# Modulation matmuls in a decoder step: column strips taken four at a time

## The chip, the cores and the metric

The kernel runs as one program on one core of a Trainium2 chip. Its time is device microseconds from a timed run; three runs were made of the kernel before. One further execution was profiled, and all rows below come from that one.

## The reference, cut to what matters

A two-layer decoder step runs on 1024 prompt tokens and 8 sample tokens. Layer 0 mixes tokens by retention and by an attention that is restricted to the highest index scores; layer 1 by a gated delta rule. Each layer has an MLP. Each sub-layer's input and output are modulated by vectors that depend on nine conditioning rows (one of the prompt, eight of the samples):

```python
sc = jax.nn.silu(c)
for l in range(DEPTH):                      # DEPTH = 2
    mod = (sc @ p['ada_w'][l] + p['ada_b'][l])[:, None, :]
    sh_m, sc_m, gt_m, sh_f, sc_f, gt_f = jnp.split(mod, 6, axis=-1)
```

`ada_w[l]` is 1024 x 6144 in fp32, so a layer's modulation reads 25.2 MB of weights to make 9 x 6144 numbers. The shift and scale of the first mixer are needed before anything else; the other four of layer 0 by the end of its mixer, and all six of layer 1 by the end of the first MLP.

## The kernel before, in words

Features lie on partitions and tokens on the free axis. Every projection goes through `mm3` (L185), which multiplies exact high and low parts of the weights and of the input: three matrix products for each of 8 (or 4) slices of the contraction, over three blocks of tokens, `BLK` (384, 384 and 264 columns). `_one` makes one block of a tile of 128 output features; `dense` runs over tiles, either block by block (`blk_major`) or tile by tile.

The modulation is made in the background by a generator, `ada` and `_ada` (L313 to L339). A group g of 2048 output columns has 16 half slices of the weights, each of 128 x 1024 (512 KB), loaded by SyncE (L320) into a ring of tiles. The stationary operand is the 32-column tile `scT` of the conditioning rows. So a product with 512 moving columns fills only a strip of 32 columns of the array and 32 partitions of the PSUM bank `ps`; the four strips of a bank are the four 512-column parts of the group. Each `next` on the generator emits one load and the two strips of the load before it. An fp32 strip shows in the trace as two matmul records, so a step is four records. After the last slice the bank is copied (L330), turned (L333) and added to the bias (L339).

Where the steps go is set by the tile-by-tile branch of `dense`:

```python
if b < self.pace:
    next(self.back, None)
```

`pace` is 3 from the even mixer on, so a step follows each block. Three stretches of the kernel run these steps. In the set-up, group 0 of layer 0 runs with nothing else, over a ring of six tiles. In the even mixer's projections (`even_proj`), groups 1 and 2 of layer 0 run between the blocks of the projections AK, AV, two heads of AQ, and the first retention head's RQ, RK, RV and RG, over a ring of two tiles, `N[6]` and `N[12]`; what is left is emitted by `drain` in the middle of `ret_head` (L988). In the first MLP, all three groups of layer 1 run between its blocks, over a ring of three tiles.

The program text is not the order of the queues: a planner in the framework lists the instructions by their place in the text and by when it expects their inputs, and puts each on its engine's queue; each engine then runs its queue in that order and waits where an input is late. SyncE's queue holds the weight loads (L172), the modulation loads, the half swaps of the rotary step (L720, L721) and the spills of the residual (L399).

Other users of the tiles that the change touches: `N[11]` is `on`, which holds the rectified index scores (L844 to L851) and later the outputs of `ret_head`; `N[13]` is `scr` in the sample scores (read by L1280) and `sall`, the retention states, in `ret_head`. Both are ring tiles of the input norm before that. `N[6]` is part of the residual until it is spilled. The search for the highest index scores (`search_init`, L1149 to L1219) runs on VectorE and ScalarE along with the projections, two of its steps emitted after each tile.

Of the kernel before, what the change touches and what calls it, by code (L numbers as in the profile page):

```python
# [44 lines left out]
def _constants():  # L45
    """Tables that follow from the shapes alone."""
# [51 lines left out]
class _Ring:  # L98
    """Tiles handed out in turn."""
# [15 lines left out]
class _Carve:  # L115
    """Small tiles out of one."""
# [15 lines left out]
class _Step:  # L132
    def __init__(self, nc, tc, a, taps=None, stop=None):
        self.nc, self.tc, self.a, self.taps, self.stop = nc, tc, a, taps, stop
        self.ahead, self.pace, self.back, self.under, self.jobs = 1, 1, iter(()), [], []
        self.lanes, self.beat = ([], []), 0
# [5 lines left out]
    # ---------------------------------------------------------------- helpers  # L142
# [5 lines left out]
    def consts(self, i, t):  # L148
        """Load the constants of part i (0 everywhere, 1 even mixer, 2 odd mixer) into tile t."""
        c0, c1 = _CUTS[i], _CUTS[i + 1]  # L150
        self.cst[i] = t[:, :c1 - c0]
        self.nc.gpsimd.dma_start(self.cst[i], self.a['cst'][:, c0:c1])
# [4 lines left out]
    def banks(self, **kw):  # L157
        """Name PSUM banks by role for the code that follows."""
# [19 lines left out]
    def mm3(self, out, w, ms, X, ks, c0, c1, start=True, stop=True):  # L178
        """out[m, c0:c1] of W^T X with W and X as exact high and low parts."""
# [12 lines left out]
    def dense(self, tiles, blk_major, X=None, ks=range(8), after=None):  # L192
        """tiles: (load, m, evac); evac(block, psum). Block by block, after(block) follows each block."""
# [11 lines left out]
        else:  # L205
            self.settle()
            for t in tiles:
                w, off = t[0]()
                for b in range(3):
                    self._one(w, off, t[1], t[2], b, X, ks)  # L210
                    if b < self.pace:
                        next(self.back, None)
                    self.work(1 + b // 2)

    def work(self, n=1 << 30):
        """Emit n steps of the jobs in line."""
# [5 lines left out]
    def tick(self):  # L222
        """Emit a step of one of the two lanes in turn."""
# [6 lines left out]
    def finish(self, g):  # L230
        """Emit all of the lane of g up to its end."""
# [5 lines left out]
    def drain(self):  # L237
        """Emit what is left of the work in the background."""
# [10 lines left out]
    def rsqrt(self, out, x, n, m, scr=None):  # L249
        """out = x ** -0.5 for x [n, m] (a first guess from the bits of x, then Newton's method)."""  # L250
# [10 lines left out]
    # ---------------------------------------------------------------- set-up  # L261
# [17 lines left out]
    def vectors(self):  # L279
        """Per-feature vectors laid on partitions: ada_b (2 x 48), ln_g, ln_b (2 x 2 x 8 each) and others."""  # L280
# [3 lines left out]
        nc.sync.dma_start(ab, a['ada_b'].rearrange("l (j p) -> (l j) p", p=128))  # L284
        nc.sync.dma_start(gn[64:68], a['ret_gn'][0])
        nc.sync.dma_start(gn[68:69], a['odd_gn'])
        nc.sync.dma_start(cw, a['odd_conv'][0].rearrange("w (j p) -> (w j) p", p=128))
        nc.sync.dma_start(gn[0:32], a['ln_g'].rearrange("l s (j p) -> (l s j) p", p=128))
        nc.sync.dma_start(gn[32:64], a['ln_b'].rearrange("l s (j p) -> (l s j) p", p=128))
# [16 lines left out]
    def ada(self, l, gs, ring):  # L306
        """Modulations 2g and 2g+1 of layer l for g in gs, features on partitions, one column per conditioning
        row; a generator, a step to a load."""
# [4 lines left out]
    def _ada(self, l, g, ring):  # L313
        nc = self.nc
        ps = self.side('a')
        raw = {}
        for i in range(17):
            if i < 16:
                raw[i] = ring()
                nc.sync.dma_start(raw[i], self.a['ada_w'][l, 64 * i - i % 2 * 64:64 * i - i % 2 * 64 + 128,  # L320
                                                          2048 * g + i % 2 * 1024:2048 * g + i % 2 * 1024 + 1024])
            if i:
                kt, hf = (i - 1) // 2, (i - 1) % 2
                for c in range(2):
                    j = 2 * hf + c
                    nc.tensor.matmul(ps[32 * j:32 * j + 32, :], self.scT[:, kt, :],  # L326
                                     raw[i - 1][:, 512 * c:512 * c + 512], start=kt == 0, stop=kt == 7)
# [6 lines left out]
        # column block of (quarter q, sub j) is 16 g + 4 q + j  # L334
# [9 lines left out]
    def coefs(self, l_ln, s_ln, l, i):  # L344
        """hf = n * HS + HB with HS = g (1 + scale), HB = b (1 + scale) + shift; resid = n * RA + RB."""
# [18 lines left out]
    # ---------------------------------------------------------------- norm and modulation  # L364
    def weave(self, n):
        """Emit n steps of the norms that are under way."""
# [5 lines left out]
    def settle(self, b=2):  # L372
        """Emit all of the norms up to block b."""
# [3 lines left out]
    def spread(self, b, ns, co, to_dram, ring):  # L377
        """Natural token tiles ns of block b -> resid^T and the split modulated input XH, XL; in steps."""
# [22 lines left out]
    def spread_samples(self, v, co):  # L401
        """v [128, 8, 8], the samples with features on partitions -> resS and the last columns of XH, XL."""
# [14 lines left out]
    def normed(self, b, ring, out, final):  # L417
        """Token tiles of block b of the residual sum, normalised, tokens on partitions; in steps."""
# [44 lines left out]
    def normed_samples(self, ring, then):  # L463
        """The samples' residual sum, normalised, features on partitions; in steps."""
# [42 lines left out]
    def final_samples(self, v):  # L507
        """The samples' normalised rows, scaled, out."""
# [30 lines left out]
    # ---------------------------------------------------------------- residual sum of a projection  # L539
# [22 lines left out]
    def out_proj(self, w, l, after):  # L562
        """resid + (1 + gate) * (X^T w), X the mixer's output."""
# [11 lines left out]
    # ---------------------------------------------------------------- MLP  # L575
# [52 lines left out]
    def arena(self, cp):  # L628
        """The tiles that every phase takes its own from."""
# [8 lines left out]
    def renew(self, x, slots, dt=F32):  # L638
        """Tiles of slots of x anew: what holds float32r parts holds nothing else."""
# [9 lines left out]
    def ev_rings(self):  # L649
        """Tiles of a norm and of the MLP."""  # L650
# [9 lines left out]
    # ---------------------------------------------------------------- whole step  # L660
    def run(self, stop=None):
        nc, tc, a = self.nc, self.tc, self.a
        with tc.tile_pool(name='cp', bufs=1) as self.cp, tc.tile_pool(name='sm', bufs=2) as self.sm, \
# [17 lines left out]
            for _ in range(6):  # L681
                next(self.back)
            self.vectors()
# [3 lines left out]
            for l in range(2):  # L687
# [17 lines left out]
                if l == 0:  # L705
                    self.back = self.ada(1, range(3), _ring(*[t[:, :1024] for t in N[8:10] + [W[9]]]))
# [7 lines left out]
    # ---------------------------------------------------------------- even mixer  # L714
    def rope(self, raw, tabs, half, out, sw=None):
        """out = raw * cos + (halves of raw swapped) * signed sin."""
# [9 lines left out]
    def natural(self, src, out, tag, scale=None, rows=128):  # L726
        """src [rows, >= 1024] (features on partitions) -> out [128, 8, rows] (tokens on partitions)."""
# [14 lines left out]
    def sample_rows(self, src, out, tag, rows=128, scale=None):  # L742
        """The sample columns of src -> out [8, rows]."""
# [22 lines left out]
    def even_proj(self, mis, w, S, SS, aqS, akS, avS, aqD, akD, vD):  # L766
        """Projections, index scores, retention and the search; returns its tiles, the soonest free first."""
# [4 lines left out]
        adw = _ring(N[6], N[12])  # L772
        self.back, self.pace = self.ada(0, (1, 2), adw), 3
# [32 lines left out]
        # indexer queries, keys and weights  # L806
# [28 lines left out]
        # index scores of the prompt rows that have more than 256 keys  # L835
# [19 lines left out]
        # indexer keys out  # L855
# [9 lines left out]
        def aq_tile(h):  # L865
            """A head of queries, turned and sent to DRAM block by block."""
# [44 lines left out]
        # retention  # L911
# [42 lines left out]
    def ret_head(self, h, qT, kT, vT, vn, kn, rg, sall, on):  # L954
        """Retention of the prompt for a head, in steps."""
        nc = self.nc
        vv, kk = [x[:, :NP].rearrange("p (c r) -> p c r", c=8) for x in (vn, kn)]
# [30 lines left out]
        self.drain()  # L988
# [1016 lines left out]
```

## Time and profile before

| what | value |
|---|---|
| three timed runs | 3057.4, 3058.06 and 3073.36 us; median 3058.06 |
| span of the profiled execution | 3055.5 us |
| TensorE busy, share of the span | 2971.4 us, 97% |
| VectorE busy | 1665.6 us, 55% |
| modulation weights read | 96 loads of 512 KB |

The span runs from the first to the last instruction of the profiled execution; the median of the timed runs is 2.6 us above it. Busy time of TensorE is a sum over records whose ends are modelled and which overlap, so 97% busy does not mean that it streams columns 97% of the time.

### The profile page before, as it was taken

The numbers are of one execution on the slowest core, as the hardware profiler recorded it, in microseconds if no ns is written. First come the engines' busy times: TensorE is split into PE (matmuls) and PEld (weight loads), VectorE is DVE, ScalarE is ACT, GpSimd is POOL, SyncE is SP. The second block draws the span as 40 slices with busy tenths as digits, with TensorE's granted clock in tenths as the row PEclk, the third lists the DMA queues.
The fourth block names the chain that finished last, engine by engine and source line by source line (L and its number), as shares of the span: only waits on it lengthen the run. The fifth ranks groups of instructions, "written<-read, shape, count | busy, mean of one in ns | idle before, by whom it ended". The sixth has DMA issues, their size and how long they took to land.

```text
span 3055.5 us, 49859 instructions
## 1 busy us (share of the span) xinstructions
PE 2971.4 (97%) x20052; PEld 2736.0 (90%) x20052; DVE 1665.6 (55%) x4531; ACT 1093.7 (36%) x2240; POOL 188.6 (6%) x248
## 2 busy tenths in 40 slices
PE   8999999999999999999999999999999999999997
PEld 5577997898679999999888999999999999999996
DVE  4678895447223333333677766765575333333337
ACT  4467724425021112222365555552243221112221
POOL 0300003000000000000011111111000000000002
PEclk9999999999999999999999999998999999999998
DMA  8664226102642111111132222233311111111111
GB/s 290 187 184 145 85 78 202 48 28 63 188 156 73 49 49 43 48 49 43 52 91 52 56 54 56 51 115 109 124 56 42 43 48 49 46 45 49 44 40 63
DMA packets 257908, 251.59 MB, mean 82 GB/s; under 512 B 46262, under 2 KB 227291, under 8 KB 257164
## 3 DMA queue, kind: packets, MB, share of 16 engines
q1 hardware_dynamic: 243596, 200.38, 22.2%
q0 software_dynamic: 14080, 48.03, 4.9%
q8 instruction: 157, 2.57, 0.3%
q14 instruction: 75, 0.61, 0.1%
HBM read 207.23 MB, written 37.92 MB: 80 GB/s over the span
## 4 chain that ended last, share of the span: by engine, by line
PE 78%; DVE 11%; ACT 3%; DMA 3%; issue 3%; POOLq 0%; SPq 0%; POOL 0%; DVEq 0%; ACTq 0%
PE bank L185 63%; PE bank L326 3%; DVE wlo L174 1%; DVE W L1471 1%; PE bank L1326 1%; PE bank L1312 1%; PE bank L1839 1%; PE bank L386 1%; ACT whi L173 1%; PE bank L1523 1%; DVE st L437 1%; DMA N<-gcD 1%; DVE N L1530 1%; ACT N L450 1%; PE bank L1633 1%
## 5 line engine op out<-in xcount | busy, mean ns | idle before, releaser
L185 PE MATMUL bank<-XH,whi 128*128 128x384 f32 (+3 forms) x2832 | 942.9, 333 | 5.3 <-ACT whi L173 1.6
L185 PE MATMUL bank<-XL,whi 128*128 128x384 f32 (+3 forms) x2832 | 919.7, 325 | 0.0
L185 PE MATMUL bank<-XH,wlo 128*128 128x384 f32 (+3 forms) x2832 | 919.2, 325 | 0.0
L185 PEld LDWEIGHTS bank<-XH,whi 128*128 128x128 f32 (+2 forms) x2832 | 535.5, 189 | 37.0 <-issue 16.1
L185 PE MATMUL bank<-W,whi 128*128 128x384 f32 (+1 forms) x2304 | 543.0, 322 | 11.6 <-DVE N L593 7.3
L185 PEld LDWEIGHTS bank<-XH,wlo 128*128 128x128 f32 (+2 forms) x2832 | 534.8, 189 | 8.7 <-issue 5.9
L185 PEld LDWEIGHTS bank<-XL,whi 128*128 128x128 f32 (+2 forms) x2832 | 535.9, 189 | 7.2 <-issue 3.9
L550 DVE SCALAR_TENSOR_TENSOR N<-bank,G,N 128x384 f32<-128x384 f32 (+1 forms) x432 | 247.0, 572 | 497.9 <-PE bank L185 497.9
L185 PEld LDWEIGHTS bank<-W,whi 128*128 128x128 f32 x2304 | 394.5, 188 | 40.7 <-DVE N L550 15.7
L173 ACT CAST whi<-raw 128x1024 fp32r<-128x1024 f32 x166 | 172.7, 1040 | 674.4 <-PE bank L185 655.4
L185 PE MATMUL bank<-W,wlo 128*128 128x384 f32 (+1 forms) x1152 | 367.3, 319 | 0.0
L174 DVE TENSOR_TENSOR wlo<-raw,whi 128x1024 fp32r<-128x1024 f32 x166 | 202.7, 1221 | 145.1 <-ACT whi L173 135.8
L593 DVE SCALAR_TENSOR_TENSOR N<-bank,N 128x384 f32<-128x384 f32 (+1 forms) x192 | 98.4, 513 | 295.9 <-ACT N L592 295.7
L592 ACT ACTIVATE N<-bank 128x384 f32<-128x384 f32 (+1 forms) x192 | 87.5, 456 | 368.8 <-PE bank L185 368.8
L185 PEld LDWEIGHTS bank<-W,wlo 128*128 128x128 f32 x1152 | 216.3, 188 | 0.0
L185 PE MATMUL bank<-W,W 128*128 128x384 f32 (+1 forms) x768 | 180.8, 322 | 0.0
L185 PE MATMUL bank<-XH,W 128*128 128x384 f32 (+1 forms) x480 | 155.5, 324 | 1.2 <-DVE N L593 1.2
L185 PE MATMUL bank<-XL,W 128*128 128x384 f32 (+1 forms) x480 | 154.5, 322 | 0.0
L185 PE MATMUL bank<-XH,N 128*128 128x384 f32 (+1 forms) x480 | 154.3, 321 | 0.0
L185 PEld LDWEIGHTS bank<-W,W 128*128 128x128 f32 x768 | 132.4, 188 | 8.6 <-DVE N L550 5.0
L185 PE MATMUL bank<-W,N 128*128 128x384 f32 (+1 forms) x384 | 123.2, 321 | 0.0
L1157 ACT ACTIVATE N<-N,M 128x384 bf16<-128x384 f32 (+3 forms) x128 | 106.2, 830 | 31.1 <-DVE M L1154 27.1
(582 smaller groups left out, 3903.9 us busy)
## 6 DMA issues: line engine op xcount, KB each, us to landing
N<-in_ada_w_dram SPq DMA_DIRECT2D x64, 512.0 KB, 3.8
raw<-in_mlp_up_dram SPq DMA_DIRECT2D x64, 512.0 KB, 4.0
raw<-in_mlp_down_dram SPq DMA_DIRECT2D x64, 512.0 KB, 3.3
W<-in_ada_w_dram SPq DMA_DIRECT2D x32, 512.0 KB, 4.9
raw<-in_odd_w_in_dram SPq DMA_DIRECT2D x32, 512.0 KB, 4.1
raw<-in_even_w_in_dram SPq DMA_DIRECT2D x24, 512.0 KB, 6.3
N<-resD SPq DMA_DIRECT2D x16, 512.0 KB, 4.2
resD<-N SPq DMA_DIRECT2D x4, 1536.0 KB, 7.2
```

The lines of the kernel that those rows point to most:

```text
L173: nc.scalar.copy(hi[:, :k * m], raw[:, :k * m])
L174: nc.vector.tensor_tensor(lo[:, :k * m], raw[:, :k * m], hi[:, :k * m], op=OP.subtract)
L185: self.nc.tensor.matmul(out, ww[:, i, ms], xx[:, c0:c1], start=start and i == 0 and j == 0, stop=stop and i == nk - 1 and j == 2)
L326: nc.tensor.matmul(ps[32 * j:32 * j + 32, :], self.scT[:, kt, :], raw[i - 1][:, 512 * c:512 * c + 512], start=kt == 0, stop=kt == 7)
L386: nc.tensor.transpose(ps[:, 128 * i:128 * i + 128], n[:, 128 * ft:128 * ft + 128], self.ident)
L437: nc.vector.bn_stats(st[:, i, :], zs[i])
L450: nc.scalar.activation(x[:, y], zz[j][i], AF.Identity, scale=rs[:, j:j + 1], bias=nb[:, j:j + 1])
L550: nc.vector.scalar_tensor_tensor(r, ps[:, :w], g[:, dt, 0:1], r, op0=OP.mult, op1=OP.add)
L592: nc.scalar.activation(r, ps[:, :w], AF.Relu)
L593: nc.vector.scalar_tensor_tensor(h, ps[:, :w], 0.0, r, op0=OP.max, op1=OP.mult)
L1157: nc.scalar.activation(ja[:, :n], S[r], AF.Sign, bias=nff[:, r - 2:r - 1], accum_out=cnt[:, r - 2:r - 1])
L1312: nc.tensor.matmul(p[:, :kw], q[:, h], akT[:, k0:k0 + kw], start=True, stop=True)
```

## The change

A step of the generator now takes a whole slice of 128 rows: it emits the four strips of the bank, of two loaded tiles, and the two loads of a later slice. A group has 8 such steps in place of 16. The last strip is emitted first, and the other three are put behind it on the engine's queue. The ring is filled ahead, by half as many slices as it has tiles. `dense` counts slices of contraction and takes a step whenever `every` of them have passed: 8 in the even mixer (a step for each block, as before), 24 in the MLP (a step for each tile of `mlp_up`, and for every two of `mlp_down`). The rings have four tiles in the even mixer (`N[6]`, `N[12]`, `N[11]`, `N[13]`) and four in the MLP. `drain` moves from the middle of `ret_head` to its start. `vectors` becomes a generator whose six small loads are issued by ScalarE, ahead of the first modulation steps, and whose transposes follow after three of them. The rest of the diff removes comments.

```diff
     def dense(self, tiles, blk_major, X=None, ks=range(8), after=None):
...
-                    if b < self.pace:
+                    self.since += len(ks)
+                    if self.since >= self.every:
+                        self.since = 0
                         next(self.back, None)
...
     def vectors(self):
-        nc.sync.dma_start(ab, a['ada_b'].rearrange("l (j p) -> (l j) p", p=128))
...
+        nc.scalar.dma_start(ab, a['ada_b'].rearrange("l (j p) -> (l j) p", p=128))
...
+        yield
         p = self.side()
...
     def _ada(self, l, g, ring):
         nc = self.nc
         ps = self.side('a')
-        raw = {}
-        for i in range(17):
-            if i < 16:
-                raw[i] = ring()
-                nc.sync.dma_start(raw[i], self.a['ada_w'][l, 64 * i - i % 2 * 64:64 * i - i % 2 * 64 + 128,
-                                                          2048 * g + i % 2 * 1024:2048 * g + i % 2 * 1024 + 1024])
-            if i:
-                kt, hf = (i - 1) // 2, (i - 1) % 2
-                for c in range(2):
-                    j = 2 * hf + c
-                    nc.tensor.matmul(ps[32 * j:32 * j + 32, :], self.scT[:, kt, :],
-                                     raw[i - 1][:, 512 * c:512 * c + 512], start=kt == 0, stop=kt == 7)
+        raw = []
+
+        def load(kt):
+            raw.append([ring(), ring()])
+            for hf in range(2):
+                nc.sync.dma_start(raw[kt][hf], self.a['ada_w'][l, 128 * kt:128 * kt + 128,
+                                                               2048 * g + 1024 * hf:2048 * g + 1024 * hf + 1024])
+        n = len(ring.t) // 2
+        for kt in range(n):
+            load(kt)
+        yield
+        for kt in range(8):
+            def strip(j):
+                return nc.tensor.matmul(ps[32 * j:32 * j + 32, :], self.scT[:, kt, :],
+                                        raw[kt][j // 2][:, 512 * (j % 2):512 * (j % 2) + 512], start=kt == 0, stop=kt == 7)
+            with self.tc.issue_after(strip(3).ins):
+                for j in range(3):
+                    strip(j)
+            if kt + n < 8:
+                load(kt + n)
             yield
...
             self.back = self.ada(0, (0,), adw)
-            for _ in range(6):
+            vectors = self.vectors()
+            next(vectors)
+            for _ in range(4):
                 next(self.back)
-            self.vectors()
+            for _ in vectors:
+                pass
             self.drain()
...
                 if l == 0:
-                    self.back = self.ada(1, range(3), _ring(*[t[:, :1024] for t in N[8:10] + [W[9]]]))
+                    self.back, self.every = self.ada(1, range(3), _ring(*[t[:, :1024] for t in N[8:11] + [W[9]]])), 24
...
-        adw = _ring(N[6], N[12])
-        self.back, self.pace = self.ada(0, (1, 2), adw), 3
+        adw = _ring(*[t[:, :1024] for t in (N[6], N[12], N[11], N[13])])
+        self.back = self.ada(0, (1, 2), adw)
...
     def ret_head(self, h, qT, kT, vT, vn, kn, rg, sall, on):
         nc = self.nc
+        self.drain()
...
         nc.gpsimd.dma_start(self.a['ret_prompt'][0, 0, h], sall[:, 7])
-        self.drain()
```

## Rows read from the trace of the kernel before

**Rows 1.** The page, part 1 (busy time) and part 4 (chain that ended last).
```profile
PE 2971.4 (97%) x20052; PEld 2736.0 (90%) x20052; DVE 1665.6 (55%) x4531; ACT 1093.7 (36%) x2240; POOL 188.6 (6%) x248
...
PE 78%; DVE 11%; ACT 3%; DMA 3%; issue 3%; POOLq 0%; SPq 0%; POOL 0%; DVEq 0%; ACTq 0%
```
**Rows 2.** Windows of L326 alone, even mixer and first MLP: window, length, PE busy (records).
```profile
90.00:293.00 203.00, 34.70 (x128) 4.74 (x128) 1.00 0.60 178
755.00:940.00 185.00, 51.54 (x192) 7.04 (x192) 1.00 0.54 168
```
**Rows 3.** Timeline of TensorE round one step in the even mixer: start, length, instruction.
```profile
89.99 0.34 PE L185 MATMUL bank<-XH,wlo 128*128 128x384 f32 x1
90.25 1.05 PE L326 MATMUL bank<-N,scT 128*32 128x512 f32 x4
91.24 0.39 PE L185 MATMUL bank<-XH,whi 128*128 128x264 f32 x1
91.46 0.29 PE L185 MATMUL bank<-XL,whi 128*128 128x264 f32 x1
```
**Rows 4.** Windows of L185 alone: MLP with steps, MLP without: PE (x) PEld (x).
```profile
771.43:930.79 159.36, 119.73 (x685) 107.00 (x684) 1.00 0.55 172
1186.30:1277.80 91.50, 90.99 (x576) 90.67 (x576) 1.00 0.16 47
```
**Rows 5.** The same window of L326 alone.
```profile
771.43:930.79 159.36, 45.24 (x172) 6.19 (x172) 1.00 0.55 172
```
**Rows 6.** Chain in 755 to 945 us, shares by line.
```profile
by line: PE bank L185 74.1%; PE bank L326 25.3%; PE bank L333 0.7%
```
**Rows 7.** Windows: PE, PEld, DVE, ACT, POOL busy (x), clock, DMA share, GB/s.
```profile
90.00:166.00 76.00, 74.14 (x300) 36.86 (x300) 45.43 (x85) 35.85 (x72) 25.91 (x46) 1.00 0.59 184
166.00:292.00 126.00, 125.65 (x740) 98.58 (x738) 105.74 (x299) 91.77 (x198) 4.37 (x9) 1.00 0.60 174
292.00:440.00 148.00, 142.06 (x931) 137.52 (x928) 136.58 (x446) 74.54 (x166) 7.29 (x10) 0.97 0.28 79
440.00:482.00 42.00, 41.65 (x299) 41.27 (x297) 34.29 (x108) 12.56 (x27) 8.50 (x13) 1.00 0.48 141
```
**Rows 8.** Timeline of TensorE where two steps fall together, in the drain.
```profile
269.70 1.07 PE L326 MATMUL bank<-N,scT 128*32 128x512 f32 x8
270.69 0.49 PE L996 MATMUL bank<-W,W 128*128 128x128 f32 x2
```
**Rows 9.** DMA in 166 to 265 us: packets, the hardware queue, then L320's landings.
```profile
DMA packets 10791, 16.91 MB, mean 171 GB/s; under 512 B 792, under 2 KB 7712, under 8 KB 10784
...
q1 hardware_dynamic: 10112, 14.70, 53.0%
...
N<-in_ada_w_dram SPq DMA_DIRECT2D x18, 512.0 KB, 4.3
```
**Rows 10.** DMA in 10 to 40 us (set-up).
```profile
DMA packets 4885, 10.17 MB, mean 339 GB/s; under 512 B 387, under 2 KB 2696, under 8 KB 4884
...
W<-in_ada_w_dram SPq DMA_DIRECT2D x10, 512.0 KB, 6.1
```
**Rows 11.** Last uses of the new ring tiles: VectorE's index-score line, TensorE's L1280.
```profile
L851 DVE SCALAR_TENSOR_TENSOR N<-N,M,N x30: 350/750/753, 105.0 to 142.8; 128x512 f32<-128x512 f32 x18, 128x384 f32<-128x384 f32 x6, 128x128 f32<-128x128 f32 x3, 128x256 f32<-128x256 f32 x3
...
161.53 1.04 PE L1280 MATMUL bank<-N,N 32*32 32x512 f32 x2
```
**Rows 12.** Windows of the set-up, columns as in rows 7.
```profile
10.00:20.00 10.00, 6.47 (x27) 1.12 (x25) 0.97 (x9) 0.00 (x0) 0.00 (x0) 0.87 0.91 291
20.00:30.00 10.00, 9.25 (x34) 1.13 (x28) 0.00 (x0) 0.04 (x1) 0.00 (x0) 0.79 1.02 406
30.00:40.00 10.00, 6.53 (x26) 5.29 (x27) 6.42 (x13) 5.76 (x10) 0.00 (x0) 0.72 0.95 320
```
**Rows 13.** Timeline of TensorE in the set-up.
```profile
18.20 8.01 PE L326 MATMUL bank<-W,scT 128*32 128x512 f32 x24 [2.11 <-DMA W<-in_ada_w_dram]
```
**Rows 14.** SyncE's queue: L320's waits (ns min/median/max), and two issues in order.
```profile
L320 SPq EVENT_SEMAPHORE  x90: 17/17/6437, 11.1 to 926.4; - x90
...
91.35 0.39 SPq L320 DMA_DIRECT2D N<-in_ada_w_dram  x1
...
98.15 0.44 SPq L172 DMA_DIRECT2D raw<-in_even_w_in_dram  x1
```

More of the change, by code (lines that the diff above doesn't have):

```diff
@@ L134, in __init__ @@
         self.nc, self.tc, self.a, self.taps, self.stop = nc, tc, a, taps, stop
-        self.ahead, self.pace, self.back, self.under, self.jobs = 1, 1, iter(()), [], []
+        self.ahead, self.every, self.since, self.back, self.under, self.jobs = 1, 8, 0, iter(()), [], []
         self.lanes, self.beat = ([], []), 0
@@ L283, in vectors @@
         ab, gn, cw = [self.W[9][:n, 128 * i:128 * i + 128] for i, n in enumerate((96, 69, 96))]
-        nc.sync.dma_start(ab, a['ada_b'].rearrange("l (j p) -> (l j) p", p=128))
[L285 to L289, printed above, removed]
+        nc.scalar.dma_start(ab, a['ada_b'].rearrange("l (j p) -> (l j) p", p=128))
+        nc.scalar.dma_start(gn[64:68], a['ret_gn'][0])
+        nc.scalar.dma_start(gn[68:69], a['odd_gn'])
+        nc.scalar.dma_start(cw, a['odd_conv'][0].rearrange("w (j p) -> (w j) p", p=128))
+        nc.scalar.dma_start(gn[0:32], a['ln_g'].rearrange("l s (j p) -> (l s j) p", p=128))
+        nc.scalar.dma_start(gn[32:64], a['ln_b'].rearrange("l s (j p) -> (l s j) p", p=128))
+        yield
         p = self.side()
```

## The prediction
> **What bounds the kernel now.** I read the page first. TensorE is busy 97% of the span and holds 78% of the chain that ended last; VectorE holds 11% [rows 1]. So the question is whether TensorE is the bound in the stretches where the modulation runs, and what it spends there on modulation. L326 outside the set-up is 128 records in 90 to 293 us and 192 in 755 to 940 us [rows 2]; four records are a step, so 32 and 48 steps.
>
> The timeline shows what a step is [rows 3]. The four records are two strips in two passes. They fill 90.25 to 91.24, 0.99 us, in which the dense products stand still. Dense products follow each other every 91.50 / 576 = 0.159 us in a stretch without steps [rows 4]. From the start of the last dense product before the step (89.99) to the second after it (91.46) are 1.47 us, in which two would have needed 0.32: the step costs 1.15 us. A check over a long stretch: 159.36 us hold 172 records of L326 [rows 5], 43 steps, and 684 dense products (as many as weight loads) [rows 4]; 159.36 - 684 x 0.159 = 50.6 us, or 1.18 per step, with two tails of groups (turning and copying) in it. I take 1.15.
>
> Then the chain. In 755 to 945 us it holds TensorE alone: 74.1% dense products, 25.3% L326, 0.7% the turning [rows 6]. There nothing but TensorE sets the pace. In the even mixer it is less clean. In 166 to 292 us TensorE is busy 125.65 of 126 us, but VectorE already 105.74, or 84%; in 292 to 440 us VectorE is busy 136.58 of 148, 92%, and TensorE falls to 142.06, 96%; after 440 us TensorE is full again, VectorE at 82% [rows 7]. The search for the highest scores is what fills VectorE there.
>
> **What four strips cost.** The kernel before has run four strips together: in the drain two steps fall together, and their eight records fill 269.70 to 270.69 [rows 8], 0.99 us again. Two further strips cost less than the last digit shown, so I put a four-strip step at 1.16 us. The lower bound is 1.15, the two-strip step; the upper is the two pairs one after the other, 1.15 + 0.99 = 2.14. One event stands for the lower end and nothing for the upper, so I stay near the lower.
>
> **The first MLP.** 48 steps become 24: 48 x 1.15 - 24 x 1.16 = 55.2 - 27.8 = 27.4 us off a chain of TensorE alone. What covers the loads: a step asks for 1 MB, and steps come one per 72 dense products, 11.5 us, with two slices loaded ahead. The even mixer's loads of 512 KB land in 4.3 us [rows 9], so they are there in time; uncovered, each would cost at most that wait. The steps reach through four chunks of the MLP and end long before their results are wanted. I count the 27.4 in full.
>
> **The even mixer.** 32 steps become 16: 36.8 - 18.6 = 18.2 us of TensorE time. Three things can take from it.
>
> First VectorE. Its work does not change, so a stretch can shrink until VectorE is as full as it is seen anywhere, 92%. 166 to 292 us can go from 126 to 105.74 / 0.92 = 115 us, 11 us less, although TensorE would give back nearly all of the 18.2 there. 292 to 440 us can give nothing. Before 166 us VectorE is busy 45.43 of 76 us and lets all pass; five steps stand there, and 5 x 1.15 less two or three four-strip steps is 2.9 us. Together 14 us. The lower bound is 0: the search that is not done behind the modulation is done later, in the full stretch. The upper is 18.2: over 90 to 482 us VectorE has 322 us of work in 392, and 322 in 374 would still be only 86%, and the search may slip into the stretch after 440 us.
>
> Second the DMA queues. The step rate per block stays and each step loads twice as much. In 166 to 265 us 18 modulation loads (9.4 MB) are part of 16.9 MB at 171 GB/s, the hardware queue 53% busy [rows 9]; 9.4 MB more in that time makes 266 GB/s, against 339 GB/s that the set-up carries [rows 10]. Loads then land in 6.1 us in place of 4.3 [rows 10, 9]. Two slices ahead are two blocks of about 5 us, so this is covered, barely; what it costs where it isn't is the difference, 2 us a step, up to 30 us over the 15 steps, but the planner can also put dense products ahead of such a step. I take 0 here and let the range hold some.
>
> Third the new tiles. The second slice cannot be loaded before the last index score is read (142.8 us) and L1280 has read `scr` (161.5 + 1.0 us) [rows 11]. So one step is done before about 165 us and 15 after it, where the kernel before had done five two-strip steps. Dense products take their place, since TensorE has tiles of AK, AV and AQ to go on with; nothing is lost if only SyncE does not stand still for it (below). The moved `drain` then has nothing left to emit: 18 steps of the generators end within the first six tiles.
>
> **The set-up.** 16 steps become 8, but the stretch is a stream of loads: DMA share 0.91, 1.02 and 0.95 in three windows of 10 us [rows 12]. The run of 24 records from 18.20 takes 8.01 us [rows 13] at a granted clock of 0.79, in part at the lower of the two levels, 1.2 GHz, and it holds back the loads behind it; half of the steps could free 3 us. The six small loads leave SyncE's queue. Since the queues are full, I take 1 us, between 0 and 3.
>
> **Sum.** 27.4 + 14 + 1 = 42.4. The profiled execution becomes 3055.5 - 42.4 = 3013.1; the median of the timed runs is 2.6 us above its span, which gives 3016.
>
> **Rivals.**
>
> *The even mixer gives nothing.* VectorE or the loads hold it, and only the MLP and the set-up gain: 3058 - 28 = 3030. For it speaks VectorE's 92%; against it that TensorE is full in 166 to 292 us while VectorE waits for 16% of it.
>
> *Strips do not run side by side in a stream of steps.* The event of [rows 8] is the only one, and a planner that puts other products between the strips takes it away. At the upper bound each of the 40 steps outside the set-up costs 0.99 more, 40 us: 3016 + 40 = 3056, no change. Half of it, strips that overlap in part, gives 3036. The Trainium skill (TensorE: Matmul & The Clock Gate, Measured speedup vs the span model) has 3.07 for four tiles in place of 4, by which a four-strip step would last 1.30 of one strip's time; taken on the 0.99 us that is an estimate of 0.30 us more for each of 40 steps, and a time of 3028. The trace's one event, 0.99 us for four strips as for two [rows 8], does not show it.
>
> *SyncE's queue is held by the loads into the new tiles.* This is the one on the other side. Once a wait has held this queue for 6.4 us [rows 14], so it can happen. If the planner put the loads for `N[11]` and `N[13]` where the second load stood before, at 91.35 us [rows 14], SyncE would stand until 162.5, 71 us, and behind it wait the next weights (98.15 us) and all rotary swaps. Two tiles of weights are loaded ahead, 2 x 72 x 0.159 = 23 us, so TensorE would lose 48 to 71 us, and the time be 3064 to 3087. It decides against the change (over 3073) from 58 us of uncovered standing on. Against it: the planner lists a load when it expects its tile to be free, and the median of L320's waits is 17 ns [rows 14].
>
> **How the numbers follow.** The likeliest case, most of both savings, I give 0.58; its own range is 3007 (all 18.2 and 3 in the set-up: 3058 - 48.6 = 3009, and 2 of spread) to 3024. The even mixer without gain (3024 to 3034) 0.20; strips in part or not overlapping (3028 to 3056) 0.07; SyncE held (3030 to 3087) 0.08; what I have not thought of, to both sides, 0.07. The range 3005 to 3036 holds the first two and some of the others, a little over 0.8. Half a per cent, 15 us, is about what a measurement of this kernel can tell from no change. Faster than 3042.8 come the first two cases, most of the third and half of the fourth and fifth: 0.89. Within the bound 0.06, slower 0.05.
>
> **What would show it.** L326 outside the set-up should have the same 320 records in 40 stops, eight to a stop and each stop about 1 us; stops of four, or of 1.3 us and more, make the strips' step wrong. In the MLP the time from its first modulation step to the last chunk should fall by 27 us with TensorE alone in the chain. In the even mixer, the time from 166 us to the attention shows what VectorE left of 18 us: its share should rise above 84%, and TensorE's waits for L174 or the rotary lines should grow. SyncE's wait at the second slice's load shows whether the queue was held. The prediction is wrong if the even mixer gets longer, or if loads show up as what a modulation step waits for.

## The result and the profile after

The changed kernel takes 3029.07 us in the median of four runs (3023.77 to 3040.97), the kernel before, run beside it, 3060.9. The ratio on record is 0.9884, interval 0.9851 to 0.9917 (the quotient of the two medians is 0.9896): the medians lie 31.8 us apart, where 42 were forecast. The profiled execution is the slowest of the four (span 3039.3 us), so its own difference to the profile of before is only 16.2 us. The page, parts 1 and 4:

```profile
PE 2935.7 (97%) x20052; PEld 2741.8 (90%) x20052; DVE 1663.1 (55%) x4531; ACT 1092.1 (36%) x2240; POOL 188.5 (6%) x248
...
PE 74%; DVE 13%; ACT 4%; DMA 4%; issue 4%; POOLq 0%; SPq 0%; POOL 0%; ACTq 0%; DVEq 0%
```

TensorE has 36 us less to do than in [rows 1], with as many instructions, and its share of the chain falls from 78% to 74%. The modulation product is now L332 and its load L324. Windows of L332 alone, even mixer and first MLP:

```profile
60.00:250.00 190.00, 17.70 (x128) 2.66 (x128) 0.94 0.70 212
760.00:1110.00 350.00, 26.61 (x192) 3.91 (x192) 1.00 0.36 113
```

The same 128 and 192 records as in [rows 2] take half the time. TensorE's timeline round one step of the MLP:

```profile
805.82 0.28 PE L185 MATMUL bank<-W,N 128*128 128x264 f32 x1
806.03 0.62 PE L332 MATMUL bank<-W,scT 128*32 128x512 f32 x1
806.04 0.62 PE L332 MATMUL bank<-N,scT 128*32 128x512 f32 x2
806.05 1.03 PE L332 MATMUL bank<-W,scT 128*32 128x512 f32 x2
806.49 0.60 PE L332 MATMUL bank<-N,scT 128*32 128x512 f32 x2
806.51 0.59 PE L332 MATMUL bank<-W,scT 128*32 128x512 f32 x1
807.03 0.62 PE L185 MATMUL bank<-W,whi 128*128 128x384 f32 x2
```

Eight records in 1.00 us, the four strips of a pass within 0.02 us of each other. In the chain of 765 to 1125 us the modulation's share is

```profile
by line: PE bank L185 92.8%; PE bank L332 6.9%; PE bank L344 0.4%
```

6.9% of 360 us, 25 us, where [rows 6] had 25.3% of 190, 48 us.

To see where time came and went I count the dense products of L185 from the first and compare when the k-th starts; the count is made from the two traces and shown by no view of the profile:

```
product  what ends about there          before     after   difference
0        the set-up                        36.1      38.2     +2.1
216      index queries and keys            81.2      82.8     +1.6
360      (in the even projections)        156.5     136.7    -19.8
432                                       177.1     189.6    +12.5
1296                                      370.4     374.3     +4.0
1728     the even projections             466.8     469.1     +2.3
1800     the attention                    596.9     605.2     +8.3
2664     (before the MLP's steps)         760.0     769.5     +9.5
5000     (after the MLP's steps)         1189.5    1169.2    -20.2
14256    the last products               2977.4    2960.9    -16.5
```

The MLP gains 29.7 us. In the odd layer, which the change leaves alone, 3.7 us go again. The even projections end up with nothing, after a swing from 20 us early at product 360 to nearly 20 us late by product 670, and the attention gives back 6. The swing has its place between 130 and 190 us. Windows of the changed kernel (columns as in [rows 7]):

```profile
130.00:141.00 11.00, 8.37 (x25) 3.37 (x23) 8.59 (x15) 7.39 (x15) 5.12 (x9) 1.00 0.49 145
141.00:162.00 21.00, 19.02 (x45) 7.26 (x46) 6.53 (x14) 4.58 (x8) 5.04 (x7) 0.51 0.33 91
162.00:177.00 15.00, 13.39 (x66) 7.61 (x64) 5.98 (x18) 6.68 (x13) 3.63 (x5) 1.00 0.36 118
177.00:245.00 68.00, 63.61 (x405) 47.28 (x406) 56.15 (x165) 47.65 (x106) 4.20 (x7) 0.97 0.89 282
```

and what TensorE waited for there, from its timeline:

```profile
142.98 1.06 PE L1286 MATMUL bank<-cst,W 128*64 128x128 f32 x4 [4.31 <-DMA W<-pages]
...
177.27 1.92 PE L332 MATMUL bank<-N,scT 128*32 128x512 f32 x16 [1.80 <-DMA N<-in_ada_w_dram]
...
185.53 1.93 PE L332 MATMUL bank<-N,scT 128*32 128x512 f32 x8 [2.07 <-DMA N<-in_ada_w_dram]
```

Between the step at 91.83 and the two at 177.27 there is no modulation step. TensorE comes to the sample scores (L1286) before the cache pages are there and stands 4.3 us, from 138.67 to 142.98. Its clock falls inside that wait: up to 141 us the granted clock is 1.00, in the 21 us from there 0.51, the lower level, 1.2 GHz, where [rows 7] has 1.00 up to 292 us. In the kernel before, the same product (there L1272) starts at nearly the same time, without a wait:

```profile
142.05 1.36 PE L1272 MATMUL bank<-cst,W 128*64 128x128 f32 x8
```

SyncE meanwhile holds the second slice's loads; its timeline and what it waited for:

```profile
99.25 41.11 SPq L172 DMA_DIRECT2D raw<-in_even_w_in_dram  x5
151.34 20.86 SPq L324 DMA_DIRECT2D N<-in_ada_w_dram  x2
174.44 0.47 SPq L734 DMA_DIRECT2D W<-W  x1
```

```profile
SPq L324 <- PE bank L1294: 20.1, 1, 20.1
```

L1294 is the last reader of `scr` (L1280 in [rows 11]). So three things stand close together: the late tile, the wait for pages and the fall of the clock. The experiments take them apart.

### The profile page after: what moved, and what is told of

The parts are those of the page before. It is cut to its first block, busy times and chain, and to the rows that moved or that the text cites. A ratio compares the mean times of both kernels' runs of the same rounds, so it can differ in the third digit from the quotient of the medians.

```text
span 3039.3 us, 49868 instructions
## 1 busy us (share of the span) xinstructions
PE 2935.7 (97%) x20052; PEld 2741.8 (90%) x20052; DVE 1663.1 (55%) x4531; ACT 1092.1 (36%) x2240; POOL 188.5 (6%) x248
## 4 chain that ended last, share of the span: by engine, by line
PE 74%; DVE 13%; ACT 4%; DMA 4%; issue 4%; POOLq 0%; SPq 0%; POOL 0%; ACTq 0%; DVEq 0%
PE bank L185 60%; DVE wlo L174 1%; PE bank L332 1%; PE bank L1340 1%; DVE W L1485 1%; ACT N L1171 1%; PE bank L1326 1%; DMA N<-in_ada_w_dram 1%; PE bank L1853 1%; PE bank L397 1%; ACT whi L173 1%; PE bank L1537 1%; DVE st L448 1%; DVE N L1160 1%; DMA N<-gcD 1%
## 5 line engine op out<-in xcount | busy, mean ns | idle before, releaser
L185 PE MATMUL bank<-XH,whi 128*128 128x384 f32 (+3 forms) x2832 | 942.7, 333 | 5.7 <-ACT whi L173 2.0
L185 PE MATMUL bank<-XL,whi 128*128 128x384 f32 (+3 forms) x2832 | 920.6, 325 | 0.0
L185 PE MATMUL bank<-XH,wlo 128*128 128x384 f32 (+3 forms) x2832 | 920.1, 325 | 0.0
L185 PEld LDWEIGHTS bank<-XH,whi 128*128 128x128 f32 (+2 forms) x2832 | 536.4, 189 | 29.3 <-issue 16.0
L185 PE MATMUL bank<-W,whi 128*128 128x384 f32 (+1 forms) x2304 | 540.8, 321 | 10.4 <-DVE N L604 6.1
L185 PEld LDWEIGHTS bank<-XH,wlo 128*128 128x128 f32 (+2 forms) x2832 | 535.9, 189 | 11.5 <-issue 8.7
L185 PEld LDWEIGHTS bank<-XL,whi 128*128 128x128 f32 (+2 forms) x2832 | 536.7, 190 | 7.8 <-issue 4.4
L185 PEld LDWEIGHTS bank<-W,whi 128*128 128x128 f32 x2304 | 395.7, 188 | 23.7 <-DVE N L604 10.8
L185 PE MATMUL bank<-W,wlo 128*128 128x384 f32 (+1 forms) x1152 | 367.2, 319 | 0.0
L185 PEld LDWEIGHTS bank<-W,wlo 128*128 128x128 f32 x1152 | 216.3, 188 | 0.0
L185 PE MATMUL bank<-W,W 128*128 128x384 f32 (+1 forms) x768 | 180.0, 321 | 0.0
L185 PE MATMUL bank<-XH,W 128*128 128x384 f32 (+1 forms) x480 | 155.9, 325 | 1.2 <-DVE N L604 1.2
L185 PE MATMUL bank<-XL,W 128*128 128x384 f32 (+1 forms) x480 | 155.1, 323 | 0.0
L185 PE MATMUL bank<-XH,N 128*128 128x384 f32 (+1 forms) x480 | 154.7, 322 | 0.0
L185 PEld LDWEIGHTS bank<-W,W 128*128 128x128 f32 x768 | 132.8, 188 | 2.7 <-DVE accS L566 1.9
L185 PE MATMUL bank<-W,N 128*128 128x384 f32 (+1 forms) x384 | 123.3, 321 | 0.0
```

Source lines behind the costliest of these rows:

```text
L185: self.nc.tensor.matmul(out, ww[:, i, ms], xx[:, c0:c1], start=start and i == 0 and j == 0, stop=stop and i == nk - 1 and j == 2)
```

## The experiments

Theories for the even mixer's missing 14 us: **A**, the new tiles come free late, and what follows from it (SyncE stands, TensorE runs out of work, its clock falls) eats the gain; **B**, the DMA queues are full when steps load twice as much; **C**, VectorE's search sets the pace whatever TensorE does. Ratios are to the kernel before, with 95% intervals.

**The changed kernel again.** No edit.

> The changed kernel once more, for an interval and a second profile. Nothing is tested by it but the spread. Its first profile puts the set-up 2 us later, the even mixer's projections level with before, the attention 6 us longer, the first MLP 29.7 us shorter. If the attention's 6 us are the changed kernel's own they come again; if they belong to that one execution, this profile ends 5 to 12 us sooner. Time 3023 to 3035, ratio 0.988 to 0.992.

3036.77 us, ratio 0.9911 (0.9887 to 0.9936). The MLP gains 29.7 again, and the attention takes 6 us more again; the clock falls at 140 us again, for longer, and product 1728 is 8.3 us late (late and early are always against the same product of the kernel before).

**The MLP alone.** The set-up and the even mixer are those of before.

```diff
-self.back = self.ada(1, range(3), _ring(*[t[:, :1024] for t in N[8:10] + [W[9]]]))
+self.back, self.every = self.ada4(1, range(3), _ring(*[t[:, :1024] for t in N[8:11] + [W[9]]])), 24
```

> Only the first MLP takes four strips at a time (four ring tiles, a step every 24 slices); set-up and even mixer are as before. All theories: 24 steps of 1.15 us fewer on a chain of TensorE alone, 27 to 30 us faster, ratio 0.990 to 0.992. If it gains much less than 27, the MLP pays for something that the alignment of its dense products did not show; if the whole change gains less than this, the even mixer and the set-up lose.

3030.89 us, 0.991 (0.988 to 0.994); the MLP gains 29.7. As fast as the whole change by the timed runs.

**The even mixer alone.** The generator of four strips, the ring of four tiles and the moved `drain`, nothing else.

> Only the even mixer takes four strips at a time, over the ring of four tiles; set-up and first MLP are as before. Theory A (the tiles N[11] and N[13] come free late, SyncE stands, TensorE runs out of dense products and its clock falls), theory B (the loads at twice the rate fill the DMA queues) and theory C (VectorE is the bound) all expect no gain from the first profile: 0 to 8 us slower, ratio 1.000 to 1.003. The prediction's own account expected 14 us faster, 0.9955.

3062.21 us, 0.9997 (0.9976 to 1.0018): the even part gives nothing.

**Tiles that are free.** The changed kernel, with index scores and sample scores in a scratch tile of the search, so that `N[11]` and `N[13]` are not late.

```diff
+        xs = _ring(N[1][:, 0:512], N[1][:, 512:1024])
-                    x = on().rearrange("p c e -> p (c e)")
+                    x = xs()
-        self.sample_scores(ep, iqT, ikT, iwn, SS, (vn_, kn_), scr)
+        self.sample_scores(ep, iqT, ikT, iwn, SS, (vn_, kn_), N[1])
```

> The changed kernel, but the rectified index scores and the sample sums use N[1], the scratch of the search, so that N[11] and N[13] are free from the end of the input norm on. Nothing is left out. Theory A: the second slice loads at about 80 us, steps run between 90 and 166 us as before, SyncE does not stand at 140 to 172 us, and the projections end 8 to 18 us sooner: ratio 0.983 to 0.986 to the kernel before. Theory B: steps still wait for loads at twice the rate, gain under 5 us over the changed kernel. Theory C: no gain, 0.989.

3026.33 us, 0.9874 (0.9851 to 0.9898). Product 1728 is 10.8 us early, at a DMA share as high as after's, and its steps wait 0.2 us for loads in all. One window of it:

```profile
166.00:210.00 44.00, 43.30 (x281) 35.40 (x279) 38.36 (x118) 31.33 (x69) 5.29 (x9) 1.00 0.88 279
```

That speaks against B.

**And the small loads back on SyncE.** The kernel of the last experiment with `vectors` as before.

> The freed tiles of the run before, and besides the set-up's small vector loads and their transposes back in one piece on SyncE's queue, behind the first modulation loads. In the changed kernel the transposes of the vectors stand ahead of those of the conditioning rows on TensorE and wait for ln_b until 7.80 us, so the first modulation product starts at 9.59 us in place of 6.97. If that wait is what makes the set-up later, the first dense product comes 1 to 2.5 us sooner than with the freed tiles alone; if the set-up is bound by the stream of loads it stays within 0.5 us. In the timed runs too little to be told: ratio 0.986 to 0.989.

3027.29 us, 0.9886 (0.9857 to 0.9915). The first dense product comes 0.5 us sooner.

**A ring of two.** The changed kernel, one slice loaded ahead.

```diff
-        adw = _ring(*[t[:, :1024] for t in (N[6], N[12], N[11], N[13])])
+        adw = _ring(*[t[:, :1024] for t in (N[6], N[12])])
```

> The changed kernel with the even mixer's ring cut to its two old tiles, N[6] and N[12]: one slice ahead in place of two, and no load has to wait for the index scores or the sample sums. Theory A (late tiles): steps run from 90 us on, SyncE does not stand at 140 to 172 us, the projections end 5 to 15 us sooner than in the changed kernel. Theory B (loads): with one slice ahead each step waits longer for its loads, so the projections end as late as in the changed kernel or later, TensorE waiting on L324's loads for more than the 13.6 us of the changed kernel.

3020.45 us, 0.9871 (0.9844 to 0.9898), product 1728 11.2 us early, although its modulation products wait 5.3 us in all for loads in the even mixer, about as long as the 5.9 us of the changed kernel's first profile (the 13.6 us of the expectation take in the set-up). Fewer tiles and no late ones do better than four of which two are late.

**The second slice from GpSimd's queue.** SyncE is not held, the tile is as late as before.

```diff
-                nc.sync.dma_start(raw[kt][hf], ...
+                q = nc.gpsimd if (l, g, kt) == (0, 1, 1) else nc.sync
+                q.dma_start(raw[kt][hf], ...
```

> The changed kernel, but the two loads that wait for N[11] and N[13] (the second slice of group 1) are issued from the Pool queue, so that SyncE does not stand for them; the tiles come free as late as before. If it is SyncE's standing that costs (the rotary swaps and weights behind it), the projections end 5 to 12 us sooner than in the changed kernel. If it is the late tile itself (no modulation step to fill TensorE before 165 us, then a wait for its landing) and the clock, they end within 3 us of it.

3031.23 us, 0.9908 (0.9877 to 0.9938): no better in time than the changed kernel. In its profile TensorE stands 6.0 us for pages, and product 1728 is 6.0 us early: 8.3 us sooner than in the first profile of the changed kernel, but later than in a third one of the same program (below, 9.2 us early). So this run does not decide between SyncE's standing and the late tile.

**Half the search.** Both kernels search 16 bits of the keys in place of 32, which leaves out half of the search and so changes which keys are taken; one on the kernel with free tiles, one on the kernel before.

```diff
-            for bit in range(31, -1, -1):
+            for bit in range(31, 15, -1):
```

> The freed tiles with a search of 16 bits in place of 32, which leaves half of the search out: VectorE's load in the even mixer falls by some 55 us. Compared with the kernel before cut in the same way. If VectorE is what keeps the even mixer with freed tiles from giving all 18 us (it gives 11.8 from 81 us to the end of the projections), the two cut kernels differ by 16 to 19 us over the same dense products, and TensorE waits less than before after 230 us. If not, they differ by 12 or less.

> The kernel before with a search of 16 bits in place of 32: half of the search is left out. The pair of the cut run with freed tiles. If VectorE bounds the even mixer of the kernel before only in 292 to 440 us, its projections end some 6 to 12 us sooner than with 32 bits (the 10 us that TensorE idles there and in the stretch after); the difference of the pair is what the four-strip steps are worth where VectorE has room.

One run each: 3020.37 and 3046.36 us. From product 216 to 1728 the first needs 370.6 and the second 380.1 us: 9.5 apart, while the pair with the full search is 11.8 apart. C wanted a larger gain once VectorE had less to do; there is none. The bits that remain are searched earlier, so VectorE is still busy 89 and 87% of 166 to 292 us, which makes this a weak test of that stretch.

**Two tiles and four, side by side.** The ring of two and the unchanged changed kernel on one chip, six runs each.

> The changed kernel with a ring of two tiles in the even mixer, N[6] and N[12], beside the changed kernel itself on the same chip. If the late tiles cost what the profiles show (11 to 13 us between dense products 1728 of the two, at 455.6 us with two tiles and 469.1 with four), this one is 8 to 16 us faster in the timed runs. If the difference of the profiles is only that between executions of one kernel (the changed kernel's spans go from 3022 to 3046 us), the two medians lie within 4 us.

> The changed kernel unchanged, four tiles in the ring. If the late tiles cost what the profiles show, 8 to 16 us above the ring of two beside it, a ratio of 0.989 to 0.992 to the kernel before, and again a stretch at 1.2 GHz that begins near 140 us; if it is only the spread of executions, within 4 us of it and no such stretch.

3020.62 us, 0.9865 (0.9842 to 0.9887), against 3029.63, 0.9906 (0.9877 to 0.9935): 9 us, as theory A says. But this profile of the four tiles shows no such stretch, and its span is 3020.9 us. The windows of that execution:

```profile
130.00:141.00 11.00, 10.67 (x32) 4.33 (x33) 8.37 (x15) 8.55 (x17) 4.77 (x7) 1.00 0.45 128
141.00:162.00 21.00, 20.08 (x94) 10.23 (x93) 8.91 (x25) 7.08 (x13) 5.61 (x8) 1.00 0.39 112
162.00:177.00 15.00, 11.07 (x69) 7.81 (x68) 10.52 (x32) 7.80 (x18) 2.13 (x4) 0.89 0.90 308
177.00:245.00 68.00, 67.67 (x436) 54.52 (x436) 58.79 (x175) 49.70 (x108) 3.62 (x6) 1.00 0.80 247
```

The timelines show that the first L1286 starts without a wait, and that the first copy of a page, on GpSimd's queue, is 5.9 us earlier than in the first profile of the same program, whose row stands last; the next fence is SyncE's wait:

```profile
137.50 0.63 PE L1286 MATMUL bank<-cst,W 128*64 128x128 f32 x4
...
94.66 0.50 POOL L1244 DMA_DIRECT2D pages<-in_cache_kv_dram  x1 [2.76 <-DVE W L1256]
...
100.56 0.50 POOL L1244 DMA_DIRECT2D pages<-in_cache_kv_dram  x1 [5.77 <-issue]
```

```profile
SPq L324 <- PE bank L1294: 15.9, 1, 15.9
```

The tile is as late and SyncE stands 15.9 us, yet product 1728 is 9.2 us early. So the late tile by itself costs little: 2.0 to 2.5 us against the ring of two, which is no more than the profiles without late tiles differ among themselves (8.7 to 11.7 us early).

**Pages earlier.** The changed kernel with the page table in a tile that is free sooner, so that the copies start at 88.8 us.

```diff
+        self.gather_pages(N[5][0:1, 992:1024])
         iwn = mis(128, 9, 4)
...
-        self.gather_pages(kn_[0:1, 768:800])
```

> The changed kernel, four tiles in the ring and so the same late second slice, but the cache pages are gathered some 15 us earlier (the page table goes to a tile that is free at 78 us, so the 32 copies on GpSimd's queue start near 82 in place of 95 to 102 us). If the loss in the even mixer comes from TensorE standing for pages and the fall of its clock behind that, there is no wait for pages near 140 us, no stretch at 1.2 GHz there, dense product 1728 lies 8 to 12 us before that of the kernel before, and the timed ratio is 0.984 to 0.989, as with the ring of two. If SyncE's standing at the late tile is the loss by itself, the pages change little: ratio 0.990 to 0.993, and product 1728 within 4 us of before.

3043.84 us, 0.9945 (0.9923 to 0.9967): both theories missed. The pages start 11.8 us sooner than in the first profile after, but the planner lists the sample scores sooner too: TensorE is there at 124.6 us (132.02 less its wait) in place of 138.7, and stands longer. Its timeline, and a window:

```profile
132.02 0.85 PE L1286 MATMUL bank<-cst,W 128*64 128x128 f32 x3 [7.44 <-DMA W<-pages]
```

```profile
127.00:179.00 52.00, 45.56 (x104) 17.44 (x105) 18.07 (x33) 17.41 (x33) 8.84 (x13) 0.54 0.18 55
```

The granted clock is 0.54 for 52 us and product 1728 13.3 us late. As a cure it failed; as a dose it fits. The kernels' profiles with the full search (wait: TensorE's for pages; clock: mean of 120 to 180 us; at 1.2 GHz: (1 - clock) x 60 x 2, from the unrounded clock):

| profile | wait, us | clock | us at 1.2 GHz | product 1728 against before |
|---|---|---|---|---|
| free tiles | 0 | 1.00 | 0 | -10.8 |
| free tiles, small loads on SyncE | 0.2 | 1.00 | 0 | -8.7 |
| ring of two, first and again | 0 | 1.00 | 0 | -11.2, -11.7 |
| changed kernel beside it | 0.9 | 0.97 | 3 | -9.2 |
| even mixer alone | 6.9 | 0.94 | 7 | -3.4 |
| second slice from GpSimd | 6.0 | 0.91 | 10 | -6.0 |
| changed kernel, first profile | 4.3 | 0.83 | 20 | +2.3 |
| changed kernel again | 3.5 | 0.72 | 34 | +8.3 |
| pages earlier | 7.4 | 0.60 | 48 | +13.3 |

-10.5 us plus half of the time at 1.2 GHz gives every row within 4 us. The 3 us of the changed kernel beside the ring of two lie at 174 us, behind a wait for a modulation load. In all five profiles with a wait of 3.5 us or more, the clock falls before that wait has ended. How long it then stays low does not follow from the length of the wait, and why is open.

The timed runs bear this out. Each has on record its span and the mean granted clock of the span. Span x clock counts a microsecond at 1.2 GHz as half of one at 2.4 GHz, so it estimates what a run would have taken had the clock never fallen (too low by a few us where TensorE waited while its clock was low, as in the set-up):

| kernel | timed runs | mean time, us | mean clock | mean of span x clock, us |
|---|---|---|---|---|
| before | 55 | 3060.9 | 0.984 | 3010 |
| MLP alone | 6 | 3032.5 | 0.984 | 2981 |
| even mixer alone | 12 | 3061.5 | 0.981 | 3002 |
| changed kernel | 16 | 3032.8 | 0.979 | 2968 |
| ring of two | 12 | 3020.1 | 0.983 | 2967 |
| pages earlier | 11 | 3044.7 | 0.975 | 2966 |

The last three differ by up to 25 us in time and by 2 us in span x clock (single runs scatter by 2.5 to 5 us): what separates them is the granted clock.

## Why the prediction was right and where it failed

**Strips side by side: right.** A four-strip step is 0.996 us by the starts of its records, a two-strip step 0.983. All eight records stand together in 39 of the 40 steps; one step of the MLP is split in two. The Trainium skill (TensorE: Matmul & The Clock Gate, Measured speedup vs the span model) gives its 3.07 for four row tiles, and I had applied it to column strips, on the time of two strips, for an estimate of 0.30 us more; this trace does not agree, the two further strips cost 0.013 us. The span model of the same section of the Trainium skill, about 4 ns for each further tile, fits better: for two further strips in two passes it makes, by my estimate, 0.016 us.

**The first MLP: right, the removed steps a little too cheap.** The gain is 29.7 us in the profile after, in its repeat and in the MLP alone, where 27.4 were forecast. If a four-strip step costs the 1.16 taken, the two-strip step was (29.7 + 27.8) / 48 = 1.20 us, not 1.15; the long stretch had said 1.18, and I took the single event. No step there waits for a load.

**The even mixer: wrong.** The forecast was 14 us; alone it gives 0. By two of the prediction's own signs it failed: from product 216 to 1728 the first profile after needs 386.3 us and its repeat 392.8, where 385.6 were needed before, and modulation steps waited 5.9 and 4.4 us for loads. A third sign, VectorE's share of 166 to 292 us above 84%, came only where no tile is late: 89% with free tiles, 88% with the ring of two, 81% and 77% in the first two profiles of the changed kernel. Its three parts went differently. VectorE's limit of 11 + 2.9 us is near what the undisturbed profiles show, 9 to 12; that VectorE is what holds the rest was only argued, and half a search did not bear it out. The DMA queues were rightly put at nothing: with free tiles no step of the even mixer waits for a load. The step that failed is the third, "dense products take their place ... nothing is lost if only SyncE does not stand still". Dense products did take the place, up to product 360, 20 us early. But the stretch was gated by something else, the 32 page copies, mostly 1.16 us apart on GpSimd's queue: the sample scores start at 141.6 to 144.9 us in all profiles with the full search but the two whose copies start earlier, whether TensorE waits there or not. Without modulation steps it was there before the pages, stood, and its clock fell. I priced the missing steps as time given back, and not what TensorE would wait for once it was early. Where the tiles are not late, modulation steps remain in that stretch and the wait for pages is gone. With half of the time at 1.2 GHz taken off on both sides, products 216 to 1728 need 8 to 12 us less than before in every profile with the even part changed and the full search: the forecast 14 was mostly there, and the clock took it back.

**SyncE held: true, but cheap.** It stood 20.1 us in the first profile and 15.9 in the undisturbed one. Two steps' loads came late behind it (TensorE waited 1.80 and 2.07 us in the rows above), and TensorE shows no wait of 1 us for a rotary swap there; that is far from the 58 us from which this rival decides.

**The attention** was not in the sum. From product 1799 to 1800 it lasts 118.8 us before and 120.6 to 126.1 in the kernels with the even part changed and the full search, and goes with the granted clock of that stretch: before, the first profile after, the ring of two again and the four tiles beside it:

```profile
478.00:597.00 119.00, 112.16 (x690) 83.75 (x689) 59.40 (x187) 63.41 (x140) 22.63 (x32) 0.94 0.41 127
```
```profile
480.00:605.00 125.00, 114.73 (x689) 86.73 (x688) 60.72 (x191) 63.49 (x140) 23.16 (x33) 0.90 0.41 123
```
```profile
466.00:592.00 126.00, 116.87 (x687) 86.78 (x686) 61.13 (x191) 63.08 (x140) 23.43 (x33) 0.89 0.40 122
```
```profile
469.00:590.00 121.00, 112.94 (x690) 84.33 (x689) 59.43 (x187) 64.04 (x140) 22.64 (x32) 0.93 0.42 128
```

Why the clock falls more often there is open.

**The set-up: nothing to be seen.** Its first step starts later, at 9.59 us in place of 6.97, since the small transposes now stand ahead of it and wait for the last small load:

```profile
7.80 0.35 PE L295 MATMUL bank<-cst,W 69*128 69x69 f32 x1 [2.98 <-DMA W<-in_ln_b_dram]
...
9.59 1.93 PE L332 MATMUL bank<-W,scT 128*32 128x512 f32 x8 [0.33 <-DVE scT L277]
```

but putting them back gains 0.5 us at the first dense product. That product is 0.9 to 2.2 us later than before in the profiles with the new set-up, and between 0.3 sooner and 1.8 later in the three that keep the old one. The forecast of 1 us gained is not borne out.

**The number.** 3016 was forecast. The range held 3029 because it also held a rival, "the even mixer gives nothing" (3030). That rival describes the time best, but it names VectorE or the loads as the cause, where the runs show the clock; that its number fits is luck. The sum itself was near for a clock that does not change: span x clock falls from 3010 to 2968 us, by 42, where 42.4 were forecast (29.7 of the MLP and the 8 to 12 of the even mixer make 38 to 42). What the sum left out is that the mean granted clock falls too, from 0.984 to 0.979, which on a span of 3031 us is 15 us. Between the ring of two and the four tiles beside it the mean clocks are 0.983 and 0.980, or 9 us, which is the whole difference of their medians. Which stretch of a timed run was at 1.2 GHz its record doesn't show; in the profiles, the stretch from 140 us and the attention are where the kernels differ most.

## What to carry to other kernels

Where background work leaves a stretch that something else gates, moving foreground work forward only brings the engine to the gate earlier: ask which wait it meets there, and what the wait does to its clock. When kernels are compared, put the mean granted clock beside each time; here it separates work that is gone from time that came back. Before a ring is made longer, look at when each new tile is last read; two tiles that are free beat four of which two are late, by 9 us here. When single executions of a kernel differ by 30 us, profile it more than once before explaining a difference.

## What was not expected of the hardware

A wait of 3.5 to 7.4 us of TensorE came with 7 to 48 us at 1.2 GHz, so that, by half of the time at that level, the after-effect costs up to five times the wait (17 us behind 3.5). One program shows this stretch in two profiles and lacks it in a third (spans 3039.3, 3046.1 and 3020.9 us); in the third the page copies on another queue start 5 to 6 us earlier. Four column strips take 1.3% longer than two, in steps as in the drain of [rows 8].
